# Attention scores on one core: a straight program with hand-set semaphores in place of a scheduled one, with the first output tile laid over the first unit's input buffer

## The chip, the cores and the metric

The kernel runs on one core of a Trainium2 chip. The time is the device time of one execution in microseconds (us); the value of the kernel before is the median of three runs. The profile is one execution of the same program. Its engines are called PE (matmul; PEld is its weight load), DVE (vector), ACT (scalar), POOL (GpSimd) and SP (sync, which here issues all transfers). Lower is better.

## The reference

For 8 x 8 heads, 512 queries are multiplied with 512 keys of 64 elements, and the scores are scaled. There is no softmax and no second product.

```python
batch, heads, seq, dim = 8, 8, 512, 64          # q, k: float32
scale = 1.0 / np.sqrt(q.shape[-1])
return (np.einsum('bhqd,bhkd->bhqk', q, k) * scale).astype(np.float32)
```

The inputs are two arrays of 8.4 MB each, the output is 67.1 MB.

## The kernel before

The work is cut into four units of two batches. For each unit, k and q are loaded (2.1 MB each) into one buffer of a pool of three, cast to bf16 by POOL, transposed by PE as pairs of bf16 seen as 32-bit words (four chunks of 8 word columns per unit), and moved from PSUM to `kT` and `qz` by DVE and ACT. Each unit then makes four output tiles of 4.2 MB. A tile has 8 pairs of matmuls; each pair is one PSUM buffer of 128 x 1024 float32, which ACT and DVE in turn scale into the output buffer. The output buffers come from the same pool of three as the inputs ("big"), so the first output tile takes the buffer that the second unit's input had.

```python
big_pool = ctx.enter_context(tc.tile_pool(name="big", bufs=3))
bf_pool = ctx.enter_context(tc.tile_pool(name="bf", bufs=6))
t_pool = ctx.enter_context(tc.tile_pool(name="t", bufs=2))
tpsum_pool = ctx.enter_context(tc.tile_pool(name="tpsum", bufs=2, space=bass.MemoryType.PSUM))
psum_pool = ctx.enter_context(tc.tile_pool(name="psum", bufs=2, space=bass.MemoryType.PSUM))
# ... (cut)
def load_and_cast(v):
    xf = big_pool.tile([P, 2, 2, J * D], f32, name="big")
    both = []
    for x, src in enumerate((k_r, q_r)):
        nc.sync.dma_start(out=xf[:, x], in_=src[v].rearrange("p (s c) -> p s c", s=2))
    for x in range(2):
        xb = bf_pool.tile([P, JP, 2, D, 2], bf16, name="xb")
        wide = (1, RO)[x]
        for s in range(2):
            pinned(nc.gpsimd.tensor_copy(out=..., in_=...))      # (shortened)
        both.append(words(xb.rearrange("p j s d e -> p j (s d e)")))
    return both

def rearrange(tp, pattern, dst):          # one chunk: four copies, all on DVE or all on ACT
    nonlocal n_tp
    copy = (nc.vector.tensor_copy, nc.scalar.copy)[n_tp % 2]
    n_tp += 1
    for s in range(2):
        src = tp[half(s)].rearrange(pattern, n=N, h=2)
        for h in range(2):
            pinned(copy(out=dst(s, h), in_=src[:, h]))
            yield
# ... (cut: transpose)
def scores(v, t):
    kT, qz = ts[v]
    o = big_pool.tile([P, 2, RO, S], f32, name="big")
    for x in range(2):
        n = 2 * t + x
        for i in range(0, RO, 2):
            ps = psum_pool.tile([P, 2, S], f32, name="ps")
            for w in range(2):
                pinned(nc.tensor.matmul(out=ps[:, w, :], lhsT=qz[:, i + w, n, :],
                                        rhs=kT[:, n].rearrange("d m s j -> d (m s j)"),
                                        start=True, stop=True))
            evacuate(o[:, x, i:i + 2, :], ps)
            yield
    nc.sync.dma_start(out=out_r[v, t], in_=o.rearrange("p x i k -> p x (i k)"))
# ... (cut)
cast = [load_and_cast(v) for v in range(UNITS)]
ts = {}
for _ in transpose(0, *cast[0]):
    pass
for v in range(UNITS):
    ahead = transpose(v + 1, *cast[v + 1]) if v + 1 < UNITS else iter(())
    for t in range(TILES):
        for n, _ in enumerate(scores(v, t)):
            take(ahead, 1 if v == 0 else int(n in (0, 2, 3, 5, 6)))
```

The whole kernel stands inside the scheduler's frame (`with tile.TileContext(nc) as tc:`). The frame sets every semaphore and wait; on leaving it, it adds a closing part in which the engines wait for one another and its semaphores are cleared. In the profile the closing part has the line L195, the opening part L184, the loads L83 and the stores L146.

Of the kernel before, what the change touches and what calls it, by code (L numbers as in the profile page):

```python
# [1 line left out]

# [5 lines left out]


@with_exitstack  # L10
def kernel(
    ctx: ExitStack,
    tc: tile.TileContext,
    q: bass.AP,
    k: bass.AP,
    out: bass.AP,
):

    nc = tc.nc
    B, H, S, D = q.shape
    scale = 1.0 / (D ** 0.5)
    P = 128
    UNITS = B // 2
    N = H  # L30
    M = P // (2 * H)
    R = S // M
    J = R // 2
    RO = 8
    U = S // RO
    JP = J // 2
    JJ = J // RO // 2
    W = 8
    IW = W // JJ
    TILES = N // 2  # L40

    f32 = mybir.dt.float32
    bf16 = mybir.dt.bfloat16

    q_r = q.rearrange("(v b) g (m j) d -> v (b g m) (j d)", b=2, j=R)
    k_r = k.rearrange("(v b) g (m j) d -> v (b g m) (j d)", b=2, j=R)
    out_r = out.rearrange("(v b) (t x h) (u i) k -> v (b t) (h u) x (i k)", b=2, x=2, h=2, i=RO)

    consts = ctx.enter_context(tc.tile_pool(name="consts", bufs=1))

    big_pool = ctx.enter_context(tc.tile_pool(name="big", bufs=3))
    bf_pool = ctx.enter_context(tc.tile_pool(name="bf", bufs=6))
    t_pool = ctx.enter_context(tc.tile_pool(name="t", bufs=2))
    tpsum_pool = ctx.enter_context(tc.tile_pool(name="tpsum", bufs=2, space=bass.MemoryType.PSUM))
    psum_pool = ctx.enter_context(tc.tile_pool(name="psum", bufs=2, space=bass.MemoryType.PSUM))


    pinned = tc.keep_in_program_order

    n_evac = 0  # L60
    n_tp = 0

    def evacuate(dst, src):
        nonlocal n_evac
        if n_evac % 2 == 0:
            pinned(nc.scalar.mul(out=dst, in_=src, mul=scale))  # L66
        else:
            pinned(nc.vector.tensor_scalar(out=dst, in0=src, scalar1=scale, scalar2=None,  # L68
                                           op0=mybir.AluOpType.mult))
        n_evac += 1  # L70

    def half(h):
        return slice(h * D, (h + 1) * D)

    def words(ap):
        return ap.bitcast(f32)

    def load_and_cast(v):

        xf = big_pool.tile([P, 2, 2, J * D], f32, name="big")  # L80
        both = []
        for x, src in enumerate((k_r, q_r)):
            nc.sync.dma_start(out=xf[:, x], in_=src[v].rearrange("p (s c) -> p s c", s=2))  # L83
        for x in range(2):
            xb = bf_pool.tile([P, JP, 2, D, 2], bf16, name="xb")

            wide = (1, RO)[x]
            for s in range(2):
                pinned(nc.gpsimd.tensor_copy(  # L89
                    out=xb[:, :, s].rearrange("p (g i) d e -> p g e i d", i=wide),  # L90
                    in_=xf[:, x, s].rearrange("p (g e i d) -> p g e i d", e=2, i=wide, d=D)))
            both.append(words(xb.rearrange("p j s d e -> p j (s d e)")))
        return both

    def rearrange(tp, pattern, dst):

        nonlocal n_tp
        copy = (nc.vector.tensor_copy, nc.scalar.copy)[n_tp % 2]
        n_tp += 1
        for s in range(2):  # L100
            src = tp[half(s)].rearrange(pattern, n=N, h=2)
            for h in range(2):
                pinned(copy(out=dst(s, h), in_=src[:, h]))  # L103
                yield

    def transpose(v, kb, qb):


        kT = t_pool.tile([P, N, M, 2, J], bf16, name="kT")
        qz = qzs[v % 2]  # L110
        ts[v] = (kT, qz)
        kw = words(kT)
        qw = words(qz)
        for j0 in range(0, JP, W):
            tp = tpsum_pool.tile([P, W, P], f32, name="tp")
            for j in range(W):
                pinned(nc.tensor.transpose(out=tp[:, j, :], identity=identity, in_=kb[:, j0 + j]))  # L117
            yield
            yield from rearrange(tp, "d j (n h m) -> d h n m j",
                                 lambda s, h: kw[half(h), :, :, s, j0:j0 + W])  # L120
        for i0 in range(0, RO, IW):
            tp = tpsum_pool.tile([P, IW, JJ, P], f32, name="tp")
            for i in range(IW):
                for jj in range(JJ):
                    pinned(nc.tensor.transpose(out=tp[:, i, jj, :], identity=identity,  # L125
                                               in_=qb[:, RO * jj + i0 + i]))
            yield
            yield from rearrange(tp, "d i jj (n h m) -> d h i n m jj",
                                 lambda s, h: qw[half(h), i0:i0 + IW, :, h * U // 2:(h + 1) * U // 2]
                                 .rearrange("d i n (m s jj) -> d s i n m jj", s=2, jj=JJ)[:, s])  # L130

    def scores(v, t):

        kT, qz = ts[v]
        o = big_pool.tile([P, 2, RO, S], f32, name="big")
        for x in range(2):
            n = 2 * t + x
            for i in range(0, RO, 2):
                ps = psum_pool.tile([P, 2, S], f32, name="ps")
                for w in range(2):  # L140
                    pinned(nc.tensor.matmul(out=ps[:, w, :], lhsT=qz[:, i + w, n, :],  # L141
                                            rhs=kT[:, n].rearrange("d m s j -> d (m s j)"),
                                            start=True, stop=True))
                evacuate(o[:, x, i:i + 2, :], ps)
                yield
        nc.sync.dma_start(out=out_r[v, t], in_=o.rearrange("p x i k -> p x (i k)"))  # L146

    def take(steps, count):
        for _ in range(count):
            next(steps, None)  # L150

    identity = consts.tile([P, P], dtype=f32)
    make_identity(nc, identity)
    qzs = [consts.tile([P, RO, N, P], bf16, name=f"qz{n}") for n in range(2)]
    for qz in qzs:
        nc.vector.memset(qz, 0.0)  # L156
    cast = [load_and_cast(v) for v in range(UNITS)]

    ts = {}
    for _ in transpose(0, *cast[0]):  # L160
        pass
    for v in range(UNITS):
        ahead = transpose(v + 1, *cast[v + 1]) if v + 1 < UNITS else iter(())
        for t in range(TILES):
            for n, _ in enumerate(scores(v, t)):

                take(ahead, 1 if v == 0 else int(n in (0, 2, 3, 5, 6)))
        for _ in ahead:
            pass


# [1 line left out]
_INS = ['q', 'k']  # L173
_OUTS = [((8, 8, 512, 512), 'float32')]


# [23 lines left out]
```

## Time and profile before

| | us |
|---|---|
| time, median of 3 runs | 202.54 (202.44 to 203.04) |
| span of the profiled execution | 200.7 |
| PE busy | 105.3 (52%) |
| PE weight load busy | 45.8 (23%) |
| DVE busy | 106.8 (53%) |
| ACT busy | 85.0 (42%) |
| POOL busy | 39.5 (20%) |
| transfers: share of the 16 DMA engines' span | 98.3% |

| instruction | count | mean |
|---|---|---|
| matmul, 128x512 | 256 | 447 ns |
| scaling out of PSUM on DVE, 128x1024 | 64 | 1224 ns |
| the same on ACT | 64 | 1023 ns |
| cast on POOL, 128x2048 | 16 | 2468 ns |
| move of transposed words on DVE, 64x512 | 32 | 686 ns and 687 ns |
| the same on ACT | 32 | 577 ns and 602 ns |
| zero fill on DVE, 128x4096 | 2 | 3472 ns |

The busy shares are averages over the whole span. The times of an engine that works beside others don't add up to the span; what counts is who is waited for, and when. The lines of the page and of the trace on which the reading rests stand in the prediction.

### The profile page before, as it was taken

Reading aid. Unit: us, or ns where it says so; the run is one execution under the profiler, and the core shown is the slowest. Engines: PE = TensorE matmul, PEld = TensorE weight load, DVE = VectorE, ACT = ScalarE, POOL = GpSimd, SP = SyncE. Lnnn points to the kernel's source line nnn. Section 1 sums busy time; section 2 is a strip of 40 time slices with the busy share of each in tenths; the row PEclk is TensorE's granted clock in tenths of the full one; section 3 lists DMA queues with packets and bytes.
Section 4 is the critical chain, followed back from the end, with each engine's and each line's share of the span. In section 5 each row is a group of like instructions: output and inputs, shape, how many; then the busy total and the mean of one; then the engine's idle time right before and its main releaser. Section 6 shows DMA issues by size and latency. Waiting matters only on the chain.

```text
span 200.7 us, 1143 instructions
## 1 busy us (share of the span) xinstructions
PE 105.3 (52%) x384; PEld 45.8 (23%) x384; DVE 106.8 (53%) x98; ACT 85.0 (42%) x97; POOL 39.5 (20%) x22
## 2 busy tenths in 40 slices
PE   0035758566657465478637496748585667510000
PEld 0034535223214131224313122312121111100000
DVE  6705538486475976485749357844444444630000
ACT  2004423864755629253844384366435243620000
POOL 1299999995000000000000000000000000000000
PEclk9999576999699999957999759975858858975555
DMA  6999999999999999999999999999999999999994
GB/s 206 424 444 437 421 421 441 434 395 421 434 424 441 428 431 431 433 426 434 431 428 424 434 441 424 431 431 434 424 431 434 431 424 431 428 437 428 428 428 199
DMA packets 5509, 83.95 MB, mean 418 GB/s; under 512 B 384, under 2 KB 384, under 8 KB 384
## 3 DMA queue, kind: packets, MB, share of 16 engines
q1 hardware_dynamic: 5504, 83.89, 98.3%
q8 instruction: 3, 0.05, 0.1%
q14 instruction: 2, 0.02, 0.0%
HBM read 16.78 MB, written 67.11 MB: 418 GB/s over the span
## 4 chain that ended last, share of the span: by engine, by line
DMA 40%; DVE 10%; PE 8%; ACT 6%; issue 1%; ACTq 0%; SPq 0%; DVEq 0%
DMA out_dram<-big 40%; DVE big L68 9%; PE ps L141 8%; ACT big L66 5%; ACT qz L103 1%; DVE qz L103 1%; ACTq L66 0%; SPq L146 0%; DVEq L68 0%
## 5 line engine op out<-in xcount | busy, mean ns | idle before, releaser
L141 PE MATMUL ps<-kT,qz 128*128 128x512 bf16 x256 | 87.6, 447 | 55.5 <-ACT big L66 41.6
L68 DVE TENSOR_SCALAR big<-ps 128x1024 f32<-128x1024 f32 x64 | 78.4, 1224 | 59.8 <-PE ps L141 37.2
L66 ACT ACTIVATE big<-ps 128x1024 f32<-128x1024 f32 x64 | 65.5, 1023 | 73.0 <-PE ps L141 37.2
L141 PEld LDWEIGHTS <-qz 128*128 128x128 bf16 x256 | 27.2, 106 | 111.0 <-issue 97.5
L89 POOL CAST xb<-big 128x2048 bf16<-128x2048 f32 x16 | 38.8, 2468 | 7.9 <-DMA big<-in_k_dram 7.3
L117 PE MATMUL tp<-identity,xb 128*128 128x128 f32 x64 | 11.6, 346 | 13.4 <-POOL xb L89 13.4
L103 ACT COPY kT<-tp 64x512 f32<-64x512 f32 x16 | 9.2, 577 | 15.3 <-PE tp L117 15.1
L103 DVE COPY kT<-tp 64x512 f32<-64x512 f32 x16 | 11.0, 686 | 6.3 <-PE tp L117 6.0
L117 PEld LDWEIGHTS tp<-identity,xb 128*128 128x128 f32 x64 | 10.5, 184 | 15.2 <-POOL xb L89 13.4
L103 DVE COPY qz<-tp 64x512 f32<-64x512 f32 x16 | 11.0, 687 | 2.7 <-PE tp L125 2.5
L103 ACT COPY qz<-tp 64x512 f32<-64x512 f32 x16 | 9.6, 602 | 2.9 <-PE tp L125 2.7
L125 PE MATMUL tp<-identity,xb 128*128 128x128 f32 x64 | 9.4, 300 | 2.5 <-ACT kT L103 2.5
L125 PEld LDWEIGHTS tp<-identity,xb 128*128 128x128 f32 x64 | 8.5, 156 | 4.3 <-issue 3.3
L156 DVE MEMSET qz<- 128x4096 uint32 x2 | 6.9, 3472 | 2.5 <-PEq L184 1.7
L103 ACT ACT_TABLE_LOAD x1 | 1.3, 1283 | 0.7 <-PEq L184 0.7
masks.py:199 POOL TENSOR_SCALAR_AFFINE_SELECT identity<-identity 128x128 f32<-128x128 f32 x1 | 0.3, 292 | 0.1
masks.py:197 POOL MEMSET identity<- 128x128 f32 x1 | 0.2, 204 | 0.3 <-POOLq L184 0.3
L184 POOL MEMSET const-float32-0.0<- 128x1 f32 x1 | 0.1, 98 | 0.2 <-issue 0.2
L184 POOL MEMSET const-bfloat16-1.0<- 128x1 bf16 x1 | 0.1, 101 | 0.0
L184 POOL MEMSET const-uint8-127<- 128x1 uint8 x1 | 0.1, 101 | 0.0
L184 POOL MEMSET const-float32-1.0<- 128x1 f32 x1 | 0.1, 98 | 0.0
## 6 DMA issues: line engine op xcount, KB each, us to landing
out_dram<-big SPq DMA_DIRECT2D x16, 4096.0 KB, 20.7
big<-in_k_dram SPq DMA_DIRECT2D x4, 2048.0 KB, 18.1
big<-in_q_dram SPq DMA_DIRECT2D x4, 2048.0 KB, 22.7
```

Of the source, the lines that this page charges most:

```text
L66: pinned(nc.scalar.mul(out=dst, in_=src, mul=scale))
L68: pinned(nc.vector.tensor_scalar(out=dst, in0=src, scalar1=scale, scalar2=None, op0=mybir.AluOpType.mult))
L89: pinned(nc.gpsimd.tensor_copy(out=xb[:, :, s].rearrange("p (g i) d e -> p g e i d", i=wide), in_=xf[:, x, s].rearrange("p (g e i d) -> p ...
L103: pinned(copy(out=dst(s, h), in_=src[:, h]))
L117: pinned(nc.tensor.transpose(out=tp[:, j, :], identity=identity, in_=kb[:, j0 + j]))
L125: pinned(nc.tensor.transpose(out=tp[:, i, jj, :], identity=identity, in_=qb[:, RO * jj + i0 + i]))
L141: pinned(nc.tensor.matmul(out=ps[:, w, :], lhsT=qz[:, i + w, n, :], rhs=kT[:, n].rearrange("d m s j -> d (m s j)"), start=True, stop=True))
L156: nc.vector.memset(qz, 0.0)
L184: nc = _bacc.Bacc("TRN2", target_bir_lowering=False, num_devices=1)
```

## The change

The kernel is rewritten as a straight program: one list of instructions for each engine, with fixed buffers and semaphores that only count upward. Only the six loads of the first three units stand inside the scheduler's frame, in a critical section; then the frame is closed and compiled, and all other instructions follow behind it, so that no closing part of the frame stands at the end. The order of the buffers is chosen by hand: the first output tile lies over the first unit's input buffer, the second over the third unit's, the third over the second's. The fourth unit's loads go into the second unit's buffer. PSUM is split into one buffer for transposes and three for scores (before: two and two). The moves of each chunk are split between ACT and DVE by halves of the partitions (before: a whole chunk to one of them). The aim is a shorter beginning and end around the transfers, and a first store that depends on less.

The diff is long; this is its core. Removed lines that only set up pools, and the helper code for shapes, are cut.

```diff
-        xf = big_pool.tile([P, 2, 2, J * D], f32, name="big")
-        both = []
-        for x, src in enumerate((k_r, q_r)):
-            nc.sync.dma_start(out=xf[:, x], in_=src[v].rearrange("p (s c) -> p s c", s=2))
+    def xf(v):
+        return bigs[(0, 1, 2, 1)[v]].rearrange("p x i k -> p (x i k)").rearrange(
+            "p (x s c) -> p x s c", x=2, s=2)
+
+    def store_buffer(g):
+        return bigs[(0, 2, 1)[g % 3]]
+
+    def load(v, x):
+        nc.sync.dma_start(out=xf(v)[:, x],
+                          in_=(k_r, q_r)[x][v].rearrange("p (s c) -> p s c", s=2)
+                          ).then_inc(load_sems[2 * v + x], 16)
+
+    with tc.tile_critical(no_gpsimd_drain=True):
+        for v in range(UNITS - 1):
+            for x in range(2):
+                load(v, x)
+    tc.close()
+    tc.compile()
+
+    for x in range(2):
+        nc.sync.wait_ge(sem["ready"], 3 + x)
+        load(UNITS - 1, x)
+    for g in range(ALL):
+        nc.sync.wait_ge(sem["act"], 4 * g + 4)
+        nc.sync.wait_ge(sem["dve"], 4 * g + 4)
+        nc.sync.dma_start(out=out_r[g], in_=store_buffer(g).rearrange("p x i k -> p x (i k)")
+                          ).then_inc(store_sems[g % 3], 16)
+    for n in range(3):
+        nc.sync.wait_ge(store_sems[n], 16 * len(range(n, ALL, 3)))
 ...
+    def scores(g, p):
+        x, i = p // 4, p % 4 * 2
+        n = g % (2 * TILES) * 2 + x
+        pair = PAIRS * g + p
+        if pair >= 3:
+            pe.wait_ge(sem["act" if p % 2 else "dve"], (pair - 3) // 2 + 1)
+        for w in range(2):
+            if p == 0 and w == 1:
+                if g < 3:
+                    pe.wait_ge(sem["ready"], (2, 6, 8)[g])
+                else:
+                    pe.wait_ge(store_sems[g % 3], g // 3 * 16)
+            ins = pe.matmul(out=pss[pair % 3][:, w, :], lhsT=qz[:, n, i + w], rhs=keys[:, n],
+                            start=True, stop=True)
+        ins.then_inc(sem["pe_dve" if p % 2 else "pe_act"], 1)
+
+    pe.wait_ge(sem["ident"], 2)
+    for c in range(CHUNKS):
+        if c % 2 == 0:
+            pe.wait_ge(sem["ready"], c // 2 + 1)
+        turn(c, first[c])
+    pe.wait_ge(sem["moved"], 4 * CHUNKS)
+    for g in range(ALL):
+        c = g + CHUNKS
+        for p in range(3):
+            scores(g, p)
+        if c < ALL:
+            pe.wait_ge(sem["ready"], c // 2 + 1)
+            turn(c, tp)
+        for p in range(3, PAIRS):
+            scores(g, p)
+        if c < ALL:
+            pe.wait_ge(sem["moved"], 4 * c + 4)
 ...
+    def evacuator(engine, copy, scaled, parity, done, freed):
+        if parity:
+            for v in range(2):
+                engine.memset(qz[:, v * N:(v + 1) * N], 0.0).then_inc(sem["zeroed"], 1)
+        for c in range(CHUNKS):
+            engine.wait_ge(sem["turn"], c + 1)
+            if c == 2:
+                engine.wait_ge(sem["zeroed"], 2)
+            move(copy, c, parity, first[c])
+        count = 0
+        for g in range(ALL):
+            o = store_buffer(g)
+            for p in range(parity, PAIRS, 2):
+                x, i = p // 4, p % 4 * 2
+                count += 1
+                engine.wait_ge(done, count)
+                scaled(o[:, x, i:i + 2, :], pss[(PAIRS * g + p) % 3]).then_inc(freed, 1)
+                c = g + CHUNKS
+                if p in (1, 2) and c < ALL:
+                    engine.wait_ge(sem["turn"], c + 1)
+                    move(copy, c, parity, tp)
```

In the loops, `ready` counts finished casts (two per unit: k, then q), `turn` counts transposed chunks, `moved` counts the moves of them (four per chunk), `act` and `dve` count finished evacuations.

## The prediction

> **What bounds the kernel now.** I read the page from its slices down: the DMA row of the 40 slices, then the queue shares, then the chain that ended last. Each digit of the DMA row is the busy share of one slice of 5.0 us; the row below gives what was moved.
>
> ```profile
> DMA  6999999999999999999999999999999999999994
> GB/s 206 424 444 437 421 421 441 434 395 421 434 424 441 428 431 431 433 426 434 431 428 424 434 441 424 431 431 434 424 431 434 431 424 431 428 437 428 428 428 199
> ...
> q1 hardware_dynamic: 5504, 83.89, 98.3%
> ...
> DMA 40%; DVE 10%; PE 8%; ACT 6%; issue 1%; ACTq 0%; SPq 0%; DVEq 0%
> ```
>
> Between the first and the last slice the transfers never stop: one queue moved 83.89 MB and its packets fill 98.3% of the 16 engines' span. No compute engine is over 53% busy on the same page. The chain is DMA by 40%, all of it stores, and the compute in it is refilling of buffers behind a running store. I then asked for busy time in five stretches. Columns: stretch, its length, busy time of PE, weight load, DVE, ACT, POOL, granted clock, DMA share, GB/s.
>
> ```profile
> 0.00:4.00 4.00, 0.00 (x0) 0.00 (x0) 2.34 (x1) 1.28 (x1) 0.70 (x6) 1.00 0.53 152
> 4.00:40.00 36.00, 17.48 (x75) 11.93 (x76) 18.90 (x19) 11.93 (x17) 31.02 (x13) 0.86 1.01 431
> 40.00:42.00 2.00, 1.52 (x9) 0.71 (x8) 1.03 (x1) 1.30 (x3) 2.00 (x2) 1.00 0.93 328
> 42.00:197.00 155.00, 86.28 (x302) 33.19 (x301) 84.52 (x79) 70.51 (x78) 5.78 (x3) 0.81 1.01 431
> 197.00:201.00 4.00, 0.00 (x0) 0.00 (x0) 0.00 (x0) 0.00 (x0) 0.00 (x0) 0.50 0.26 111
> ```
>
> The rate is 431 GB/s in both long stretches. At that rate 83.89 MB take 194.6 us. So the span of 200.7 us holds only 6.1 us that is not plain moving: about 2.6 us in the first 4 us (152 of 431 GB/s), 0.5 us where loads give way to stores (2 us at 328), 2.7 us from 197 to the end (4 x 0.74, less the 0.3 us by which 201 lies beyond the span); the 0.3 us missing are rounding of the rate. That is the whole purse from which this change can be paid, unless it alters the rate. The measured 202.54 us lies 1.8 us above the span; I take that as fixed.
>
> Last come the closing instructions, by the line that leaves the scheduler's frame, and the waits of the queue that issues DMAs.
>
> ```profile
> L195 SPq EVENT_SEMAPHORE  x7: 17/28/28, 178.5 to 200.7; - x7
> L195 SPq DRAIN  x3: 7/7/7, 200.0 to 200.3; - x3
> L195 POOLq EVENT_SEMAPHORE_RANGE_CLEAR  x1: 96/96/96, 200.4 to 200.4; - x1
> ```
>
> SP's first closing drain starts at 200.0, when the last store has been confirmed; its last wait stands at 200.7. The 0.7 us between are a handshake of all engines, a clearing of the frame's semaphores, and another handshake, after the output is complete.
>
> ```profile
> SPq L146 <- DVE big L68: 152.5, 16, 17.6
> SPq L195 <- DMA out_dram<-big: 21.2, 3, 9.6
> ...
> SPq L83 <- POOL xb L89: 4.9, 1, 4.9
> ```
>
> Each store is issued after a wait for the evacuations, yet it is early: the issue table gives 20.7 us from issue to landing, and one store's 4.19 MB take 9.7 us at 431 GB/s. So a store normally stands a whole store behind the running one.
>
> **What the Trainium skill says.** "DMA: Bandwidth & Descriptors", Specifications, gives a fabric ceiling of 435 GB/s; the 431 GB/s here is within 1% of it, so I leave the rate alone. The same page, Queues, rings and completion order, says each DMA engine consumes descriptors in ring order: a store issued earlier waits behind loads issued before it. The trace agrees: the first store, issued at 36.8 us, takes no bandwidth from the last loads, and the last cast waits until 43.2 us for its q. "Runtime: NRT & Kernel Launch", The ~15 us preamble/postamble breakdown, lists a reset of all semaphores between calls by the runtime; that is why a program may count upward and leave without clearing. No line of this trace shows that part.
>
> **The change part by part.**
>
> *End.* The frame now closes after the loads' issue, so at the end SP waits for three store semaphores and stops. Removed: 0.7 us of handshakes, less a wait instruction or two at 28 ns: **-0.65 us**, all on the path, since nothing else runs after 200.0.
>
> *Start.* SP's first load went out at 0.74 us, after the opening handshake (its semaphore wait is at 0.7). Six loads now go out inside a critical section of the frame. If entering it costs SP nothing, the first load stays at 0.74. If it costs a one-way signal, the closing handshake is the measure: two handshakes and a clear in 0.7 us, so 0.2 to 0.3 us each. My mean: **+0.1 us**. The frame's closing round then lands where SP has issued its six loads (before: the sixth at 3.44 us, 0.46 long), so the others start near 4.6 us. POOL first needs data at 8.58 us, so identity (0.5 us) fits; the two zero fills of 3.47 us on DVE end near 12 us, ahead of the first query chunk at 18.5. Hidden.
>
> *Last loads.* The fourth unit's k went out at 18.33 us, after unit 0's casts. Now it needs unit 1's k casts: 8.58 + 6 x 2.47 = 23.4 us, and its q 28.3 us. The first six loads (12.6 MB, 29.2 us, plus 2.6 us of ramp) keep the queue busy to about 32 us. Slack 8.6 us for k; q is due at 36.7 and has 8.4. Cost 0.
>
> *First tile.* Before, the first tile took unit 1's buffer and waited for its casts (ACT and DVE begin at 28.13). Now it takes unit 0's. Casts of unit 0 end at 8.58 + 4 x 2.47 = 18.5; 16 transposes took 2.57 us; the last chunk's moves, split over ACT (2 x 0.60) and DVE (2 x 0.69), add 1.4: scores from 22.5. Eight pairs before took 28.1 to 36.8 with transposes between: first store near 32 us instead of 36.81. But the eight loads (16.78 MB) keep the queue until about 38.9 + 2.6 = 41.5 us. 4.8 us are won in front of a queue that is busy: **0 us**. The second tile waits, as before, for unit 2's casts (about 38) and the third for unit 3's (48.0).
>
> *Steady state.* The same 256 matmuls, 128 evacuations (1.02 and 1.22 us), 64 moves and 64 transposes. Per tile DVE has 4 x 1.22 + 2 x 0.69 = 6.3 us, ACT 5.3, PE 16 x 0.447 + 4 x 0.32 = about 8.4: under the store's 9.7 us, and two stores lie in front of a buffer's reuse. PSUM has three score buffers and one transpose buffer instead of two and two, which couples PE less to one evacuator. A tile at a store's landing now needs that landing in PE's order (the second matmul waits), so PE has half a pair ready, not two pairs: perhaps 1 us later per tile. One sample before: landing 82.96, next store issued 91.97, so 9.0 us of 19.4. Ten us to spare; 1 us changes nothing.
>
> Sum: 202.54 - 0.65 + 0.1 = **202.0 us**.
>
> **Rivals.** (a) *The closing of the frame waits for its loads.* Before, SP did wait at the frame's end for three DMA semaphores (21.2 us). If it waits for six loads now, casts start near 33 us, the fourth unit's loads go out at 48 and later, and the first store near 57: about 15 us or more of empty queue, some 217 to 220 us. Against it: the loads count on semaphores of the program's own, for which the frame has no later reader. I give it 4%. (b) *PE's in-order waits bind.* PE waits for moves, ready casts, PSUM and stores in one line. For it: PE is the longest per tile, and the clock falls to 0.5 at times. Against: it would have to grow by 10 us a tile before the queue runs dry. If it bound in the first tiles only, 203 to 205 us. (c) *The early store pays.* If the dip at 40 to 42 us came from a store issued too late, it would vanish: -0.5 us, 201.5. Against: the store was issued 3.2 us ahead of it. (d) *The frame's entry is a full round.* Then +0.7 at the start eats the gain: 202.6.
>
> **Range and chances.** The known terms lie within 0.7 us, the three runs before spread over 0.6 us (202.44 to 203.04), and the packets of the ramp can shift by about that. Range **201.2 to 202.9 us**. Faster by 2% means under 198.5: two thirds of the purse, 4.0 of 6.1 us, for which I see no source: 0.01. Slower by 2% means over 206.6, for rival (a) and a bad form of (b): 0.05. Same: 0.94.
>
> **What would show it.** Right: no clear of semaphores at the end, SP's last wait within 0.1 us of the last store's landing, that round at 4 to 5 us instead; first load issued by 0.74 to 1.1 us; first store near 32 us with a time to landing 5 us longer than before; 431 GB/s from 42 us on; the dip unchanged. Wrong: a slice under 400 GB/s in the middle (a store came late), a first cast after 9 us (entry cost or a wait for loads), or a rate that differs.

## The result and the profile after

| | before | after |
|---|---|---|
| time, median (range) in us | 202.50 (202.41 to 203.04), 6 runs | 201.45 (201.31 to 202.0), 6 runs |
| ratio to before, 95% interval | | 0.9948 (0.9937 to 0.9959) |
| span of the profiled execution, us | 200.7 | 200.1 |

The change takes 1.05 us off, half a percent. That is within 2%, as predicted, and 201.45 us lies in the range 201.2 to 202.9, but 0.55 us below the point 202.0. The span fell by 0.6 us, which is what the working gave. The other half came from a place that I had called fixed.

First the stretches of the changed kernel, in the columns of the prediction (stretch, length, busy PE, weight load, DVE, ACT, POOL, clock, DMA share, GB/s).

```profile
0.00:4.00 4.00, 0.00 (x0) 0.00 (x0) 0.00 (x0) 0.00 (x0) 0.20 (x4) 1.00 0.54 135
4.00:40.00 36.00, 14.24 (x61) 9.76 (x63) 19.13 (x17) 12.14 (x16) 31.47 (x15) 0.89 1.01 430
40.00:42.00 2.00, 2.00 (x10) 1.77 (x9) 0.78 (x1) 1.03 (x1) 2.00 (x2) 0.50 0.99 377
42.00:197.00 155.00, 83.66 (x309) 35.85 (x313) 86.16 (x81) 71.76 (x80) 5.78 (x3) 0.80 1.01 430
197.00:201.00 4.00, 0.00 (x0) 0.00 (x0) 0.00 (x0) 0.00 (x0) 0.00 (x0) 0.50 0.29 123
```

The page's two rows of transfers, one digit or number for each slice of 5.0 us:

```profile
DMA  6999999999999999999999999999999999999996
GB/s 190 439 422 429 426 442 429 422 409 426 432 436 432 422 432 432 432 429 429 432 429 432 426 439 432 432 422 439 432 429 419 426 442 429 429 419 436 429 436 259
```

The rate is 430 GB/s where it was 431, and no slice between the first and the last is under 409 GB/s. The dip from loads to stores reads 377 instead of 328 in these two microseconds, but the stretch 38 to 44 us reads 401 here and 412 before: the dip is no smaller, it only falls a little differently on the window.

Now SP's list in order of time, and the instructions of the frame's closing (L87 in this kernel).

```profile
0.95 0.39 SPq L78 DMA_DIRECT2D big<-in_k_dram  x1
...
3.53 0.46 SPq L78 DMA_DIRECT2D big<-in_q_dram  x1
23.41 0.33 SPq L78 DMA_DIRECT2D big<-in_k_dram  x1
28.31 0.33 SPq L78 DMA_DIRECT2D big<-in_q_dram  x1
31.18 147.45 SPq L96 DMA_DIRECT2D out_dram<-big  x16
```

```profile
L87 SPq EVENT_SEMAPHORE  x2: 17/17/17, 4.5 to 4.9; - x2
...
L87 POOLq EVENT_SEMAPHORE_RANGE_CLEAR  x1: 49/49/49, 4.6 to 4.6; - x1
```

The first load goes out at 0.95 us instead of 0.74; the closing round, before at 200.0 to 200.7, is over at 4.9 us, and the clear of semaphores stands in it. SP's end, by the line of its final waits (durations in ns, then first and last start in us):

```profile
L99 SPq EVENT_SEMAPHORE  x2: 17/4856/9695, 180.8 to 190.4; - x2
```

The last wait begins at 190.4 and lasts 9.695 us, to 200.1, the end of the span. Nothing follows it.

Before, the last store landed at 199.9 us and the span ended 0.8 us later; now it lands at 200.1, where the span ends. So within the span 0.2 us are lost ahead of the last landing and about 0.8 us won behind it. The first load also went out 0.2 us later, but that this is the same 0.2 us is not shown by these two traces alone: the eight loads land 0.13 to 0.24 us later than before, and the second store at the same time, 63.5 us. The experiment without a frame comes back to it. The rest of the 1.05 us must lie outside the span. For each run the time and the span are known (the span to 0.1 us). Their difference has a median of 1.77 us for the kernel before (1.74 to 1.83 in 21 later runs) and of 1.31 us after (1.26 to 1.35). That is 0.46 us, and the sum closes: +0.2 - 0.8 - 0.46 = -1.06 us.

### The profile page after: what moved, and what is told of

Its sections match the earlier page's. It is cut to its first block, busy times and chain, and to the rows that moved or that the text cites. A ratio compares the mean times of both kernels' runs of the same rounds, so it can differ in the third digit from the quotient of the medians.

```text
span 200.1 us, 1081 instructions
## 1 busy us (share of the span) xinstructions
PE 99.9 (50%) x377; PEld 47.4 (24%) x384; DVE 106.1 (53%) x98; ACT 84.9 (42%) x97; POOL 39.5 (20%) x22
## 4 chain that ended last, share of the span: by engine, by line
DMA 58%; DVE 12%; PE 10%; POOL 7%; issue 1%; SPq 0%
DMA out_dram<-big 42%; DVE big L212 10%; DMA big<-in_k_dram 8%; DMA big<-in_q_dram 7%; POOL xb L122 7%; PE ps L145 7%; PE tp L130 3%; DVE qz L184 2%; DVE kT L184 1%; SPq L78 0%; SPq L95 0%; SPq L87 0%; SPq L82 0%
## 5 line engine op out<-in xcount | busy, mean ns | idle before, releaser
L145 PE MATMUL ps<-kT,qz 128*128 128x512 bf16 x249 | 79.7, 454 | 61.9 <-DMA out_dram<-big 31.1
L212 DVE TENSOR_SCALAR big<-ps 128x1024 f32<-128x1024 f32 x64 | 76.9, 1222 | 52.3 <-PE ps L145 47.9
L145 PEld LDWEIGHTS ps<-kT,qz 128*128 128x128 bf16 x256 | 25.2, 110 | 109.6 <-DMA out_dram<-big 34.4
L130 PE MATMUL tp<-identity,xb 128*128 128x128 f32 x104 | 19.2, 347 | 13.7 <-POOL xb L122 13.7
L184 DVE COPY qz<-tp 64x512 f32<-64x512 f32 x12 | 8.3, 695 | 3.8 <-PE tp L130 3.4
L184 ACT COPY qz<-tp 64x512 f32<-64x512 f32 x12 | 7.5, 621 | 1.7 <-PE tp L130 1.6
L130 PE MATMUL ps<-identity,xb 128*128 128x128 f32 x24 | 5.6, 420 | 1.2 <-POOL xb L122 1.2
L130 PEld LDWEIGHTS ps<-identity,xb 128*128 128x128 f32 x24 | 5.0, 226 | 1.6 <-POOL xb L122 1.6
L184 DVE COPY qz<-ps 64x512 f32<-64x512 f32 x4 | 2.8, 694 | 2.1 <-PE ps L130 2.0
L184 ACT COPY qz<-ps 64x512 f32<-64x512 f32 x4 | 2.5, 625 | 2.4 <-PE ps L130 2.4
## 6 DMA issues: line engine op xcount, KB each, us to landing
big<-in_k_dram SPq DMA_DIRECT2D x4, 2048.0 KB, 15.6
```

The lines of the kernel that those rows point to most:

```text
L130: ins = pe.transpose(out=dst[:, w], identity=identity, in_=xw[:, c % SLOTS * W + w])
L145: ins = pe.matmul(out=pss[pair % 3][:, w, :], lhsT=qz[:, n, i + w], rhs=keys[:, n], start=True, stop=True)
L184: copy(out=dst, in_=src[:, h]).then_inc(sem["moved"], 1)
L212: lambda o, ps: nc.vector.tensor_scalar(out=o, in0=ps, scalar1=scale, scalar2=None, op0=mult),
```

## The experiments

All ratios are to the kernel before on the same chip. "Outside" is the median of time less span over the runs of one kernel.

**What lies outside the span.** Two explanations stood: four of the five engines have left long before the last store lands, or the frame's handshake and clear at the end cost something that comes later. The first kernel keeps the changed program and makes the other four engines stay.

```diff
+    for engine in (nc.tensor, nc.vector, nc.scalar, nc.gpsimd):
+        for n in range(3):
+            engine.wait_ge(store_sems[n], 16 * len(range(n, ALL, 3)))
```

> The changed kernel, but PE, DVE, ACT and POOL also wait for the three store semaphores at their ends, as SP does. Theory (the part of the time that lies outside the span shrinks because four of five engines have left long before the last store lands): span stays at 200.1 to 200.2 us, the part outside grows from 1.35 back to about 1.8 us, time about 201.9 us. Rival (that part shrank because no handshake and clear of the frame stand at the end): span and time as the changed kernel's, 201.45 us.

Measured: 202.03 us (201.79 to 202.35, 16 runs), ratio 0.9976 (0.9969 to 0.9984). Median span 200.2 us, outside 1.83 us (1.78 to 1.87). No handshake and no clear were added, and the outside part is back where it was. The first explanation stands; the second falls.

**The whole program back inside the frame.** The critical section now holds everything, so the frame closes at the end.

```diff
     with tc.tile_critical(no_gpsimd_drain=True):
         for v in range(UNITS - 1):
             for x in range(2):
                 load(v, x)
-    tc.close()
-    tc.compile()
-    (all that follows)
+        (all that follows, inside the section)
```

> The changed kernel's whole program inside the frame's critical section, so that the frame closes at the end. Theory (all the gain lies in the end): first load still at 0.95 us, the closing round of 0.7 us or a little more after the last landing, span about 200.9 us and time about 202.7 us, that is at or 0.2 us above the kernel before. Rival (the straight program itself moves data better): under 202.2 us.

Measured: 203.11 us (202.95 to 203.29), ratio 1.0031 (1.0020 to 1.0043): 0.3% slower than the kernel before, clear of the noise. Span 201.3, outside 1.80. Straight order and hand-set semaphores alone win nothing. The closing is longer than I expected, because the critical section has an end of its own (L82) ahead of the frame's (L238):

```profile
L82 SPq EVENT_SEMAPHORE  x3: 17/28/28, 200.3 to 200.5; - x3
```

```profile
L238 SPq EVENT_SEMAPHORE  x2: 17/17/17, 200.9 to 201.3; - x2
...
L238 POOLq EVENT_SEMAPHORE_RANGE_CLEAR  x1: 71/71/71, 201.0 to 201.0; - x1
```

From the last landing at 200.1 to 201.3 there are 1.2 us: 0.5 for the section's end, 0.7 for the frame's.

**No frame at all.** The six loads stand first in SP's list, and no scheduler is entered.

```diff
-    with tc.tile_critical(no_gpsimd_drain=True):
-        for v in range(UNITS - 1):
-            for x in range(2):
-                load(v, x)
-    tc.close()
-    tc.compile()
+    for v in range(UNITS - 1):
+        for x in range(2):
+            load(v, x)
```

> The changed kernel without any scheduler's frame: the six loads stand first in SP's list. Theory (entering the frame's critical section cost the first load 0.21 us, and every later transfer follows it): first load at 0.74 us, span 199.9 us, time about 201.25 us, no other change although the closing round at 4 to 5 us is gone. Rival (the slow packets of the first 4 us absorb a start that is 0.2 us earlier): 201.45 us.

Measured: 201.24 us (201.1 to 201.3), ratio 0.9937 (0.9925 to 0.9950); span 199.9, outside 1.30.

```profile
0.73 0.39 SPq L78 DMA_DIRECT2D big<-in_k_dram  x1
```

The first load goes out 0.22 us earlier than in the changed kernel, and the median of the time is 0.21 us lower. The two ratios' intervals overlap, and the two traces don't carry the rest: without a frame the first load lands 0.05 us earlier, the last one 0.03 us earlier and the second store 0.12 us later. What carries it are the spans of many runs. The ten runs of this kernel and of a second one without a frame (ACT alone waits, below) have 199.8 to 200.0 us, median 199.9; the 58 runs of the changed kernel and of those variants that enter the frame only for the six loads, without the one that doubles all of DVE's evacuations, have 200.0 to 200.8 us, median 200.15. So the entry's 0.2 us is paid in the span, though the scatter of single landings hides where. This is the fastest version of the study, and it beats both kernels at the median.

**The first tile's place alone undone.** Buffers and waits are in the order of before; all else is the changed kernel.

```diff
-        return bigs[(0, 1, 2, 1)[v]]...
+        return bigs[(0, 1, 2, 0)[v]]...
-        return bigs[(0, 2, 1)[g % 3]]
+        return bigs[(1, 2, 0)[g % 3]]
-        nc.sync.wait_ge(sem["ready"], 3 + x)
+        nc.sync.wait_ge(sem["ready"], 1 + x)
-                    pe.wait_ge(sem["ready"], (2, 6, 8)[g])
+                    pe.wait_ge(sem["ready"], (4, 6, 8)[g])
```

> The changed kernel with the buffers in the order of before: first tile over the second unit's input (after casts 4), second over the third unit's, third over the first buffer, where the fourth unit's loads go. Theory (the store is in a queue that is busy until 41 us anyway): first store at 36 to 37 us instead of 31.2, its landing unchanged near 53 us, time 201.45 us within 0.2. Rival (the early store pays by a smoother change from loads to stores): 201.9 us or more.

Measured: 201.36 us (201.33 to 201.42), ratio 0.9946 (0.9932 to 0.9959). SP's list:

```profile
13.50 0.33 SPq L78 DMA_DIRECT2D big<-in_k_dram  x1
18.41 0.33 SPq L78 DMA_DIRECT2D big<-in_q_dram  x1
37.38 140.74 SPq L96 DMA_DIRECT2D out_dram<-big  x16
```

The first store goes out 6.2 us later (37.38 against 31.18) and lands at the same time: 15.6 us after its issue, against 21.8 us, so at 53.0 us in both. The last load lands at 43.2 us here and 43.3 us in the changed kernel, whether the store stands behind it 6 us earlier or later; this bears out the prediction's reading that the store takes nothing from the loads ahead of it. Laying the first tile over the first unit's input is worth nothing here.

**Which engine.** Four kernels tell whether the number of late engines counts, or one of them. Each adds to the changed kernel a final wait as above, for the engines named.

```diff
+    for engine in (nc.tensor,):        # then nc.scalar; nc.gpsimd; nc.vector
+        for n in range(3):
+            engine.wait_ge(store_sems[n], 16 * len(range(n, ALL, 3)))
```

> The changed kernel, but PE alone, beside SP, waits for the stores at its end. All four together cost 0.58 us outside the span. Theory (the last engine of all to leave sets the part outside, and one late engine is enough): about 201.9 to 202.0 us if PE is the slowest to close. Rival (the part outside grows with the number of late engines): about a quarter of it, 201.6 us.

> The changed kernel, but ACT alone, beside SP, waits for the stores at its end. One late engine is enough: 201.9 to 202.0 us. Number counts: 201.6 us. If ACT closes as fast as SP: 201.45 us.

> The changed kernel, but POOL alone, beside SP, waits for the stores at its end. So far the part outside the span is 1.31 us with SP alone, 1.46 with ACT too, 1.55 with PE too, 1.83 with all five. Theory (the shares of late engines add up: ACT 0.15, PE 0.25, so 0.13 are left for POOL and DVE together): 1.31 to 1.44 us, time 201.45 to 201.6 us. Rival (the slowest single engine sets it): either POOL or DVE alone reaches about 1.8 us, time 201.95 us.

> The changed kernel, but DVE alone, beside SP, waits for the stores at its end. Shares add up: 1.31 to 1.44 us outside the span, time 201.45 to 201.6 us. The slowest single engine sets it: about 1.8 us outside for either this or POOL alone, 201.95 us.

Then PE and ACT together:

> The changed kernel, but PE and ACT, beside SP, wait for the stores at their ends. Shares add up: 1.31 + 0.15 + 0.25 = 1.71 us outside the span, time about 201.85 us. The slowest of them sets it: 1.55 us as with PE alone, 201.7 us.

And, on the kernel without a frame, SP's three final waits moved to ACT, so that SP leaves at about 178 us:

> The kernel without a frame, and SP leaves after issuing the last store; ACT alone waits for the stores. If the remaining 1.3 us outside the span are the closing of whichever engine is last, and all close alike: 201.24 us as without this. If SP is the quickest to close: up to 201.8 us. If SP is slower than ACT: under 201.1 us.

Measured:

| waits for the end | runs | time, us | ratio (95% interval) | outside, us (range) |
|---|---|---|---|---|
| SP (the changed kernel) | 6 | 201.45 | 0.9948 (0.9937 to 0.9959) | 1.31 (1.26 to 1.35) |
| SP, DVE | 5 | 201.58 | 0.9952 (0.9938 to 0.9966) | 1.38 (1.37 to 1.45) |
| SP, ACT | 5 | 201.55 | 0.9949 (0.9937 to 0.9962) | 1.46 (1.41 to 1.48) |
| ACT alone, no frame | 5 | 201.38 | 0.9940 (0.9927 to 0.9952) | 1.45 (1.43 to 1.51) |
| SP, PE | 5 | 201.74 | 0.9955 (0.9941 to 0.9968) | 1.55 (1.54 to 1.61) |
| SP, PE, ACT | 5 | 201.63 | 0.9955 (0.9942 to 0.9967) | 1.57 (1.54 to 1.63) |
| SP, POOL | 7 | 202.02 | 0.9969 (0.9958 to 0.9980) | 1.83 (1.80 to 1.88) |
| all five | 16 | 202.03 | 0.9976 (0.9969 to 0.9984) | 1.83 (1.78 to 1.87) |

The times wander with the span by 0.1 to 0.2 us; the outside parts are tighter and are to be read. They have a limit too: a run's span is known to 0.1 us, and the kernel before reads 1.77, 1.82 and 1.78 us on the three chips. So the 0.07 us between DVE and SP are not shown; ACT, PE and POOL stand apart. After the two kernels with PE and ACT alone I took the shares for additive. That fell: PE with ACT gives 1.57, not 1.71, and POOL alone gives all of the 1.83. So there is a length for each engine between its last instruction and the end of the measured time, and the slowest of those still there sets it: SP 1.31 (DVE 1.38), ACT 1.46, PE 1.55, POOL 1.83. ACT without SP gives the same 1.45 as with it. Moving the final wait off SP is therefore a loss.

What the engines do after their last instruction lies outside the trace. The Trainium skill, "Runtime: NRT & Kernel Launch", The ~15 us preamble/postamble breakdown, names a barrier that waits for all engines and resets of semaphores there. The runs fit work on each engine that is done early by an engine that leaves early, but no run shows which of it is longer on POOL.

**How much room the compute has.** The prediction said ten microseconds to spare per tile. Each of DVE's evacuations is done twice; the second waits for the first by a new semaphore, `once`.

```diff
+                if parity:
+                    scaled(o[:, x, i:i + 2, :], pss[(PAIRS * g + p) % 3]).then_inc(sem["once"], 1)
+                    engine.wait_ge(sem["once"], count)
                 scaled(o[:, x, i:i + 2, :], pss[(PAIRS * g + p) % 3]).then_inc(freed, 1)
```

> The changed kernel with each of DVE's 64 evacuations done twice (the second waits for the first), which adds 4 x 1.22 = 4.9 us of DVE work to a tile and moves no more bytes. Step of the prediction to be tried (ten us to spare per tile, so that nothing changes): 201.45 us. Rival (only what a store takes, 9.7 us, can be spent per tile in the long run; the rest is a reserve that is used up once): DVE needs 8 x 1.22 + 1.4 + gaps, about 11.5 us per tile from 48 us on, 14 tiles end near 204 us, and the last store lands 10 us later: 213 to 216 us.

Measured: 218.18 us (218.02 to 218.28), ratio 1.0769 (1.0754 to 1.0784). The page's DMA row and its chain by line:

```profile
DMA  6999999999979698969799998979796999999995
...
DVE big L215 58%; POOL xb L122 13%; PE tp L130 5%; PE ps L145 4%; DVE qz L184 4%; DMA big<-in_k_dram 4%; DVE kT L184 3%; SPq L87 0%; POOLq L112 0%; SPq L82 0%
```

Holes in the queue, and DVE in place of the stores on the chain. From the third store (62.4 us) to the twelfth (164.9 us) they are issued 11.4 us apart, as reckoned; the last four tiles, for which there are no moves left, follow 9.6 us apart. The last store goes out at 203.1 and lands 13.7 us later, not 10, because it finds another one still running. That is why the time lies above the 213 to 216 us. Then two of the four evacuations twice, by this edit to the kernel just shown:

```diff
-                if parity:
+                if parity and p in (1, 5):
...
-                    engine.wait_ge(sem["once"], count)
+                    engine.wait_ge(sem["once"], (count + 1) // 2)
```

> The changed kernel with two of DVE's four evacuations of a tile done twice, 2.4 us more DVE work per tile. With all four twice DVE had 11.5 us per tile and the time rose to 218.2 us. Theory (the bound per tile in the long run is the 9.7 us of a store): 6 x 1.24 + 1.4 + gaps, about 9.1 us per tile, just under it, so 201.45 us, at most 202 us. Rival (every addition to DVE shows, because PE and the evacuators are coupled): half of the rise before, about 209 us.

Measured: 201.48 us (201.4 to 201.75), ratio 0.9949 (0.9935 to 0.9962). The page's DMA row of this kernel; below it, for the changed kernel and then for this one, the wait of PE's weight load for a store's landing (us in total, times, longest):

```profile
DMA  6999999999999999999999999999999999999995
```

```profile
PEld ps L145 <- DMA out_dram<-big: 34.4, 12, 4.3
```

```profile
PEld ps L145 <- DMA out_dram<-big: 7.6, 7, 1.9
```

2.4 us of extra DVE work per tile cost nothing, 4.9 us cost 16.7 us in all. The limit per tile lies between, where a store's 9.7 us is. The time from a store's issue to its landing shows the reserve: the longer it stands behind another store, the more is left. With all four doubled it is 11.2 to 12.0 us for the second to the eleventh store, hardly more than a store takes alone: the reserve is spent at once. With two doubled it starts smaller than in the changed kernel (15.4 to 16.7 us for the second to sixth store, against 16.3 to 20.4) but grows again, to 21.0 us at the last store (21.9): below the limit the reserve refills.

## Why the prediction was right, and where it wasn't

- **What bounds it.** Right. 430 GB/s in both long stretches; the data's own 194.6 us did not move.
- **End, -0.65 us.** Right within 0.15: SP's end coincides with the last landing at 200.1, and about 0.8 us behind the landing are gone. Putting the program back into the frame brings the round back, and 0.5 us for the section's end besides.
- **Start, +0.1 us.** The mechanism was right (a one-way cost at the frame's entry), the size was 0.21 us: first load at 0.95 instead of 0.74. Without a frame it is 0.73, and the spans are about 0.2 us shorter.
- **"The measured 202.54 us lies 1.8 us above the span; I take that as fixed."** This step failed, by 0.46 us of the 0.55 between the point and the result. (The start cost 0.1 us more and the end won 0.15 us more than reckoned; that these two nearly cancel is luck.) The part outside is 1.31 us when only SP is late and 1.83 us when POOL is. Before, all engines left together at 200.7 us after the handshake; after, POOL has nothing to do past its casts.
- **Last loads, 0.** Right: issued at 23.41 and 28.31 us, predicted 23.4 and 28.3, ahead of a queue that stays full.
- **First tile, 0.** Right, and shown by undoing it: store at 31.18 (predicted near 32), 4.7 us longer from issue to landing than before (21.8 against 17.1), no gain.
- **"Ten us to spare" per tile.** Wrong, though nothing in the sum hung on it. I took the time between a landing and the next store, 9.0 us of 19.4, for the load of a tile on that whole interval. But the engines work through the tiles one after another, so in the long run a tile has what a store takes, 9.7 us; the rest of the 19.4 is a reserve. The same paragraph had the right measure beside it, each engine's work per tile under the store's 9.7 us: it leaves DVE 9.7 - 6.3 = 3.4 us, between the 2.4 that cost nothing and the 4.9 that did not fit. The same error stands in rival (b), which asked for ten more microseconds a tile: under five were enough for 16.7 us.
- **PE, "about 8.4" us per tile.** Misreckoned, without effect on the sum. There are 128 transposes (two lines of 64), so 8 per tile and not 4; and counts times means, about 156 us before, add up matmuls that overlap: the page has PE busy for 105.3 us. In the changed kernel PE was busy for 80.6 us and DVE for 81.0 us from 48 to 178 us, in which 14 tiles were made: about 5.8 us per tile for each. So PE is not the longest per tile, and it had more room than the prediction gave it.
- **"1 us later per tile"** did not come. From a landing to the issue of the store three later the mean of the last twelve such intervals is 8.3 us before and 7.9 us after. But for the eight tiles of these that come with moves it is 8.40 and 8.35, and for the last four, which have none, 8.1 and 6.9. So the gain stands in the tiles that have no moves to split. Three score buffers in PSUM instead of two may have brought it; that was not tried alone.
- **Rivals.** (a), a wait for the loads in the frame's closing, is excluded by the round at 4.3 to 4.9 us while the first load lands near 8.7. (b), PE's waits, did not bind: no slice in the middle is under 409 GB/s. (c), the early store, had 201.5 us, almost the measured time, and is excluded all the same, by the undone tile and by the dip. (d), a full round at the entry, is excluded by 0.21 us.

## What to carry to other kernels

When transfers fill the span and a change leaves their rate alone, only the two ends are left to improve: look at when the first load is issued, and at all that happens after the last landing. An engine with no part in the last store should be let go early, POOL first; the wait for the last store belongs on the engine that closes quickest, here SP. For a buffer ring, compare an engine's work per tile with the time of one transfer, not with the time until the buffer comes back.

## What the runs showed of the hardware that was not expected

- The measured time beyond the last instruction depends on which engine is last: 1.31 us for SP to 1.83 us for POOL, and only the slowest of those still there counts.
- A store that found the queue empty took 11.2 us from issue to landing (the fourth, sixth and tenth; the seventh 11.6) in the kernel with all of DVE's evacuations doubled. Its 4.19 MB are 9.7 us at 431 GB/s, so some 1.5 us come on top of the moving. They are hidden as soon as a second store stands behind: the last five stores of that kernel land 9.7 us apart. The Trainium skill, "DMA: Bandwidth & Descriptors", Anatomy of one DMA, fits 2.0 us plus bytes at 436 GB/s for another issuing path, an estimate of 11.6 us here; the measurement is a little below it. The view of that kernel's sixteen stores:

```profile
DMA to landing us min/median/max: 11.2/11.8/18.2
```
